# Weaving the weight tiles of three stages column by column, so that weight loads read with a step

## The chip, the cores and the metric

The kernel runs on one core of a Trainium2 chip. The metric is the time of one execution in microseconds of device time, the median of three runs. One profiled execution of the same kernel gives the trace that the views below are taken from.

Engines are named as in the profile: PE is TensorE with its matmuls, PEld is TensorE's weight loads (they overlap the matmuls), DVE is VectorE, ACT is ScalarE, POOL is GpSimd, SP is the sync engine, which issues the weight transfers.

## The reference

Two residual layers over 256 tokens of width 2048, in float32. The first has a mixer of Fourier and gated linear attention, the second a mixer of dilated attention. Each ends with a gated feed-forward part of inner width 5632, and these feed-forward parts are where the change lies:

```python
D_MODEL, SEQ, DEPTH, D_FF = 2048, 256, 2, 5632

def conv_ffn(xn, w_gate, w_up, conv_w, conv_b, w_down):
    g = xn @ w_gate
    g = lax.conv_general_dilated(g, conv_w[:, None, :], window_strides=(1,),
                                 padding=[(1, 1)], dimension_numbers=('NWC', 'WIO', 'NWC'),
                                 feature_group_count=D_FF) + conv_b
    h = jax.nn.gelu(g) * (xn @ w_up)
    return h @ w_down

def reference(x, ...):
    h = x
    for layer in range(DEPTH):
        xn = rms_norm(h, mix_norm_g[layer])
        h = h + (fourier_gla_mixer if layer % 2 == 0 else dilated_mixer)(xn, ...)
        h = h + conv_ffn(rms_norm(h, ffn_norm_g[layer]), ...)
    return h
```

## The kernel before

All weights come as one stream of tiles of 128x128 values, here called slots, in the order in which the program uses them. In device memory 16 slots lie side by side as a unit of 128 partitions x 2048 values; one transfer of 1 MB on SP's queue brings a unit into a `raw` tile. A unit is then split in two halves of eight slots each: ACT rounds a half to the short float32 format of TensorE (`hi`, line 119) and DVE takes the remainder (`lo`, line 120). So a half of eight slots is a pair of tiles `hi` and `lo` of 128 x 1024 values, and a slot is 128 neighbouring columns of each. `Stream.take` hands out a slot (or four at once) and runs the transfers and the splits ahead of use.

The stages in the order of the stream, with their slots: q0 64, z0 4, k0 64, a0 and v0 128 each, g0 128, o0 256, u0 1408 (gate and up projection of the first layer), d0 704 (down projection of the first layer), then the four blocks of q1, k1 and v1 with 768 together, o1 256, u1 1408 and d1 704 (the second layer's feed-forward part). That makes 6020 slots.

There are two kinds of matmul loop. In `mov` (stages a0, v0, q1, k1, v1) four slots of weights are the moving operand. In `stat` (all the others but z0) one slot is the stationary operand: it is loaded into the array, and the activations move. An activation operand of 128 x 512 values holds the rounded values of 256 tokens and their remainders; `pairs` reads it as columns c and c+256 in turn, that is, successive values lie 256 values (1 KB) apart. For every slot `stat` makes a matmul of `hi` with all 512 columns (line 337) and one of `lo` with the 256 columns of the rounded values (line 323). The second ones are held back in a list and sent off when the stream is at a multiple of 16 slots:

```python
                        if self.st.at % 16 == 0:
                            flush()
                        hi, lo = self.st.take(mat, k, j)
                        x = operand(k)
                        nc.tensor.matmul(ps[j], hi, self.pairs(x), start=k == k0, stop=False)
                        late.append(lower(ps[j], lo, x, k == k1))
```

So TensorE does 16 matmuls of 512 columns in a row, and then 16 of 256 columns, each with a weight load of 128 columns of its own. Stage z0 is a loop of its own (lines 462 and 463) with weight loads of 32 columns, and the attention of the second layer has matmuls whose moving operand is 256 neighbouring values (lines 895 and 936). `spread` (line 306) has a stationary operand that is one column repeated 128 times.

The order of the work is set by the order of the program and by the pools (three `raw` tiles, three `hi`, four `lo`, five accumulators). `pack` builds the stream's array ahead of the launch, outside of the time that is measured.

Of the kernel before, what the change touches and what calls it, by code (L numbers as in the profile page):

```python
# [14 lines left out]
P = 128  # L15
# [8 lines left out]
SLOT = 128  # L24
# [36 lines left out]
def slots_of(groups):  # L61
    return [(m, k, j) for m, js, ch in groups for c in ch for j in js for k in c]


def slots_of_block(mat, b):
    return [(mat, k, 4 * b + j) for k in range(KT) for j in range(4)]


def stream_slots():
    s = slots_of(Q0)  # L70
    s += [("z0", k, 0) for k in range(4)]
    s += slots_of(K0)
    for m in ("a0", "v0"):
        for b in range(2):
            s += slots_of_block(m, b)
    s += slots_of(G0) + slots_of(O0) + slots_of(U[0]) + slots_of(DN[0])
    for b in range(4):
        for m in ("q1", "k1", "v1"):
            s += slots_of_block(m, b)
    s += slots_of(O1) + slots_of(U[1]) + slots_of(DN[1])  # L80
    return s


class Stream:


# [3 lines left out]
    def __init__(self, k, src):  # L90
        self.k, self.src = k, src
        self.slots = stream_slots()
        self.at = 0
        self.halves = -(-len(self.slots) // 16) * 2
        self.raws = []
        self.ready = []
# [26 lines left out]
    def take(self, mat, kk, j, n=1):  # L123
        assert self.slots[self.at] == (mat, kk, j), (self.slots[self.at], mat, kk, j)
        half, off = divmod(self.at, 8)
        assert off + n <= 8
        if off == 0 and half > 0:
            self.k.side_step()
        while len(self.ready) < min(half + 1 + self.AHEAD, self.halves):
            self.split_next()  # L130
        hi, lo = self.ready[half]
        self.at += n
        s = slice(off * SLOT, (off + n) * SLOT)
        return hi[:, s], lo[:, s]


# [856 lines left out]
def shape_constants():  # L993
    i = np.arange(P)
    tri = np.stack([i[:, None] <= i[None], i[:, None] >= i[None], i[:, None] == i[None]], 1)
    lev = np.stack(
        [
            (i[:, None] // (2 * w) == i[None] // (2 * w)) & (i[:, None] // w != i[None] // w)
            for w in LEVELS
        ],  # L1000
        1,
    )
    n = np.arange(T)
    ang = 2 * np.pi * ((n[:, None] * n[None]) % T) / T
    cs = np.concatenate([np.cos(ang)[:, 0:129], np.sin(ang)[:, 1:128]], 1)
    dft = [m.reshape(2, P, -1) for m in (cs, np.cos(ang)[:, 0:P] / T, np.sin(ang)[:, 0:P] / T)]
    dft = np.concatenate([m.transpose(1, 0, 2).reshape(P, -1) for m in dft], 1)
    d = np.arange(512) - (T - 1)
    hot = np.arange(32)[:, None] == t5_bucket(d)[None]
    count = (np.abs(d) <= 64).astype(int) + (d % 4 == 0) + (d % 16 == 0)  # L1010
    cnt = np.where(count > 0, np.log(np.maximum(count, 1)), -1e30)
    return {
        "tri": tri.astype(np.float32),
        "lev": lev.astype(np.float32),
        "dft": dft.astype(np.float32),
        "hot": hot.astype(np.float32),
        "cnt": np.ascontiguousarray(np.broadcast_to(cnt, (16, 512))).astype(np.float32),
    }


def cols(v):

    return np.asarray(v).reshape(-1, P).T


def pack(inp):
    inp = {k: np.asarray(v) for k, v in inp.items()}
    w_in = inp["w_in_even"][0]
    w_qkv = inp["w_qkv_odd"][0]
    mirror = np.concatenate([np.arange(P), [P], np.arange(T - 1, P, -1)])  # L1030
    order = np.concatenate([g * T + mirror for g in range(4)] + [np.arange(1024, D)])
    mats = {
        "a0": w_in[:, 0:1024], "q0": w_in[:, 1024:1536], "k0": w_in[:, 1536:2048],
        "v0": w_in[:, 2048:3072], "g0": w_in[:, 3072:4096], "o0": inp["w_out_even"][0][order],
        "q1": w_qkv[:, 0:2048], "k1": w_qkv[:, 2048:4096], "v1": w_qkv[:, 4096:6144],
        "o1": inp["w_out_odd"][0], "d0": inp["w_down"][0], "d1": inp["w_down"][1],
    }
    for i in range(2):
        mats[f"u{i}"] = np.stack(
            [inp["w_gate"][i].reshape(D, FT, P), inp["w_up"][i].reshape(D, FT, P)], 2  # L1040
        ).reshape(D, 2 * FF)
    z = w_in[:, 4096:4128].reshape(4, 4, P, 32).transpose(0, 2, 1, 3).reshape(4 * P, P)
    mats["z0"] = z
    slots = stream_slots()
    w = np.zeros((-(-len(slots) // 16) * 16, P, SLOT), np.float32)
    tiles = {m: a.reshape(-1, P, a.shape[1] // P, P) for m, a in mats.items()}
    for s, (m, k, j) in enumerate(slots):
        w[s] = tiles[m][k, :, j]
    w = np.ascontiguousarray(w.reshape(-1, 16, P, SLOT).transpose(0, 2, 1, 3)).reshape(-1, P, UNIT)
    gates = np.zeros((33, 1024), np.float32)  # L1050
    gates[0:16, 0:512] = inp["gate_up_fwd"][0]
    gates[16:32, 512:1024] = inp["gate_up_bwd"][0]
    gates[32, 0:512] = inp["gate_bias_fwd"][0]
    gates[32, 512:1024] = inp["gate_bias_bwd"][0]
    par = np.concatenate(
        [
            cols(inp["mix_norm_g"]), cols(inp["ffn_norm_g"]), cols(inp["gla_norm_g"]),
            cols(inp["q_norm_g"]), cols(inp["k_norm_g"]),
        ],
        1,  # L1060
    )
    conv = np.concatenate([inp["conv_w"], inp["conv_b"][:, None]], 1)
    conv = conv.reshape(2, 4, FT, P).transpose(3, 0, 2, 1)
    x = inp["x"][0].T.reshape(KT, P, T).transpose(1, 0, 2)
    arrays = {"w": w, "gates": gates, "par": par, "conv": conv, "x": x, "rel": inp["rel_bias"]}
    arrays.update(shape_constants())
    return {k: np.ascontiguousarray(v) for k, v in arrays.items()}
# [29 lines left out]
```

## Time and profile before

| what | value |
|---|---|
| median of 3 runs | 2077.5 us (2077.2 to 2077.78) |
| the profiled execution, its own time | 2077.91 us |
| span of its trace | 2075.5 us |
| PE, PEld, DVE, ACT busy | 100%, 90%, 71%, 54% of the span |
| granted TensorE clock | 1.0 |
| weight transfers, share of 16 DMA engines | 53.9% |

The trace gives each instruction a start and an end. The ends of matmuls are modelled and overlap the next matmul, so what a matmul costs in a row of equal ones is read from one start to the next, not from its duration. Weight loads run beside the matmuls in the same way.

### The profile page before, as it was taken

How to read it: one execution, taken by the hardware profiler on the slowest of the kernel's cores; microseconds unless marked ns; L12 is line 12 of the kernel's file. 1: busy time of each engine (PE TensorE's matmuls, PEld its weight loads, DVE VectorE, ACT ScalarE, POOL GpSimd, SP SyncE). 2: the span in 40 equal slices, each digit the busy share in tenths (PEclk: the TensorE clock that was granted, in tenths of full speed). 3: DMA queues.
4: the chain of work that ended last, by engine and by line, in shares of the span. 5: the costliest groups of instructions: out<-in, count | busy, mean ns of one | idle time of the engine just before them, and what ended most of it. 6: DMA issues, size and time to landing. Idle time of an engine off the chain costs nothing.

```text
span 2075.5 us, 30467 instructions
## 1 busy us (share of the span) xinstructions
PE 2065.7 (100%) x12226; PEld 1876.8 (90%) x12226; DVE 1474.0 (71%) x2268; ACT 1125.8 (54%) x1623; POOL 22.1 (1%) x28
## 2 busy tenths in 40 slices
PE   8999999999999999999999999999999999999999
PEld 7898999999999999999888888999999999999998
DVE  7696777777777775655676777778777777765554
ACT  6765555555555554444455555556555555554443
POOL 3000000000000000000000000000000000000000
PEclk9999999999999999999999999999999999999999
DMA  7433555555555555555655455555555555555564
GB/s 273 162 142 127 198 203 188 202 202 203 203 203 203 198 200 198 200 200 202 232 184 197 178 178 188 180 192 200 201 202 203 203 203 201 199 200 211 206 212 151
DMA packets 60409, 406.28 MB, mean 196 GB/s; under 512 B 6875, under 2 KB 9435, under 8 KB 12524
## 3 DMA queue, kind: packets, MB, share of 16 engines
q1 hardware_dynamic: 56924, 398.93, 53.9%
q0 software_dynamic: 896, 3.28, 0.5%
q8 instruction: 95, 1.56, 0.3%
q10 hardware_dynamic: 2448, 2.13, 0.3%
q14 instruction: 46, 0.38, 0.0%
HBM read 402.19 MB, written 2.13 MB: 195 GB/s over the span
## 4 chain that ended last, share of the span: by engine, by line
PE 97%; ACT 1%; issue 0%; DVE 0%; DMA 0%; SPq 0%; DVEq 0%; ACTq 0%
PE acc L337 51%; PE acc L323 26%; PE acc L354 5%; PE acc L355 5%; PE acc L353 5%; PE ax L553 1%; PE ax L895 1%; PE ax L936 1%; PE ax L921 0%; PE ax L871 0%; ACT hi L119 0%; PE ax L688 0%; PE ax L621 0%; DMA raw<-in_w 0%; DVE page L254 0%
## 5 line engine op out<-in xcount | busy, mean ns | idle before, releaser
L120 DVE TENSOR_TENSOR lo<-raw,hi 128x1024 fp32r<-128x1024 f32 (+1 forms) x755 | 925.5, 1226 | 431.2 <-ACT hi L119 427.3
L337 PE MATMUL acc<-page,hi 128*128 128x512 f32 x4992 | 1136.4, 380 | 4.2 <-ACT hi L119 2.6
L119 ACT CAST hi<-raw 128x1024 fp32r<-128x1024 f32 (+1 forms) x755 | 791.9, 1050 | 510.3 <-PE acc L337 366.9
L337 PEld LDWEIGHTS acc<-page,hi 128*128 128x128 f32 x4992 | 918.6, 189 | 126.6 <-ACT hi L119 5.4
L323 PEld LDWEIGHTS acc<-page,lo 128*128 128x128 f32 x4992 | 607.2, 192 | 17.2
L323 PE MATMUL acc<-page,lo 128*128 128x256 f32 x4992 | 609.1, 275 | 0.0
L353 PE MATMUL acc<-hi,page 128*128 128x512 f32 x512 | 197.1, 385 | 0.0
L354 PE MATMUL acc<-lo,page 128*128 128x512 f32 x512 | 194.1, 379 | 0.3 <-DVE lo L120 0.3
L355 PE MATMUL acc<-hi,page 128*128 128x512 f32 x512 | 194.0, 379 | 0.0
L750 ACT ACTIVATE c<-t,conv 128x256 f32<-128x256 f32 x88 | 52.8, 600 | 155.4 <-DVE t L748 155.4
L220 ACT CAST page<-t 128x256 fp32r<-128x256 f32 x96 | 38.8, 405 | 152.3 <-DVE t L765 151.6
L355 PEld LDWEIGHTS acc<-hi,page 128*128 128x128 f32 x512 | 96.8, 189 | 13.7
L354 PEld LDWEIGHTS acc<-lo,page 128*128 128x128 f32 x512 | 96.8, 189 | 13.1 <-DVE lo L120 0.6
L353 PEld LDWEIGHTS acc<-hi,page 128*128 128x128 f32 x512 | 96.8, 189 | 12.5
L751 DVE SCALAR_TENSOR_TENSOR c<-t,conv,c 128x255 f32<-128x255 f32 x88 | 42.6, 484 | 56.3 <-ACT c L750 56.3
L362 DVE TENSOR_TENSOR t<-acc,t 128x256 f32<-128x256 f32 (+1 forms) x193 | 80.3, 417 | 0.0
L361 ACT COPY t<-acc 128x256 f32<-128x256 f32 (+1 forms) x193 | 71.0, 369 | 3.5 <-PE acc L323 2.7
L221 DVE TENSOR_TENSOR page<-t,page 128x256 fp32r<-128x256 f32 x96 | 40.6, 424 | 38.6 <-ACT page L220 38.6
L253 ACT ACTIVATE page<-hT,par 128x256 fp32r<-128x256 f32 x64 | 31.8, 506 | 38.8 <-DVE hT L729 38.2
L760 ACT ACTIVATE gr<-c 128x256 f32<-128x256 f32 x88 | 36.7, 417 | 15.7 <-DVE c L755 15.6
L755 DVE SCALAR_TENSOR_TENSOR c<-t,conv,c 128x255 f32<-128x255 f32 x88 | 42.6, 484 | 3.1
L254 DVE SCALAR_TENSOR_TENSOR page<-hT,par,page 128x256 fp32r<-128x256 f32 x64 | 34.4, 547 | 7.3 <-ACT page L253 7.3
(160 smaller groups left out, 803.0 us busy)
## 6 DMA issues: line engine op xcount, KB each, us to landing
raw<-in_w SPq DMA_DIRECT2D x373, 1024.0 KB, 4.8
raw<-in_w SPq DMA_DIRECT2D x7, 512.0 KB, 7.3
page<-brow POOLq DMA_DIRECT2D x4, 768.0 KB, 5.7
out<-hT ACTq DMA_DIRECT2D x16, 128.0 KB, 2.9
hT<-in_x SPq DMA_DIRECT2D x7, 256.0 KB, 7.4
raw<-in_w SPq DMA_DIRECT2D x2, 256.0 KB, 3.4
page<-in_dft SPq DMA_DIRECT2D x1, 512.0 KB, 6.3
page<-in_lev SPq DMA_DIRECT2D x1, 448.0 KB, 5.4
```

Of the source, the lines that this page charges most:

```text
L119: k.nc.scalar.copy(hi[:, c], part[:, c])
L120: k.nc.vector.tensor_sub(lo[:, c], part[:, c], hi[:, c])
L323: return lambda: nc.tensor.matmul(ps[:, 0:T], lo, self.pairs(x)[:, 0:P], start=False, stop=last)
L337: nc.tensor.matmul(ps[j], hi, self.pairs(x), start=k == k0, stop=False)
L353: nc.tensor.matmul(ps[t], xh, hi, start=k == 0, stop=False)
L354: nc.tensor.matmul(ps[t], xh, lo, start=False, stop=False)
L355: nc.tensor.matmul(ps[t], xl, hi, start=False, stop=k == KT - 1)
L361: self.nc.scalar.copy(v, self.unpaired(ps[0:rows, T:512]))
L362: self.nc.vector.tensor_add(v, self.unpaired(ps[0:rows, 0:T]), v)
L750: nc.scalar.activation(c, t, AF.Identity, scale=w(1), bias=w(3))
L751: nc.vector.scalar_tensor_tensor(out=c[:, 1:T], in0=t[:, 0 : T - 1], scalar=w(0), in1=c[:, 1:T], op0=ALU.mult, op1=ALU.add,)
L755: nc.vector.scalar_tensor_tensor(out=c[:, 0 : T - 1], in0=t[:, 1:T], scalar=w(2), in1=c[:, 0 : T - 1], op0=ALU.mult, op1=ALU.add,)
```

## The change

For three stages the slots that lie side by side in a half are woven in groups of g: two in u0, four in d0, eight in u1. A group of g slots takes the same g x 128 columns as before, but column c of slot i now lies at place c x g + i in the group. `places` gives for each slot the first slot of its group, the group's size and the slot's place in it. Where a stage starts or ends within a half (u1 does so with four slots at either end) the group is smaller. `take` returns for a single slot a view with a step of g values, `pack` writes the array in this order. All the other stages have groups of one, with a step of one as before. The bytes moved, the splits by ACT and DVE, which work on whole halves, and the instructions of all engines with their order are the same as before; what differs is the step with which the weight loads of lines 337 and 323 (354 and 340 in the changed file) read in u0, d0 and u1.

```diff
+WOVEN = {"u0": 2, "d0": 4, "u1": 8}
+
+def places(slots):
+    out = []
+    for s, (m, _, _) in enumerate(slots):
+        n = WOVEN.get(m, 1)
+        group = [i for i in range(s // n * n, s // n * n + n) if slots[i][0] == m]
+        out.append((group[0], len(group), s - group[0]))
+    return out
...
         self.slots = stream_slots()
+        self.places = places(self.slots)
...
         hi, lo = self.ready[half]
+        first, g, i = self.places[self.at]
         self.at += n
-        s = slice(off * SLOT, (off + n) * SLOT)
+        first = first % 8 * SLOT
+        s = slice(first + i, first + g * SLOT, g) if n == 1 else slice(first, first + n * SLOT)
         return hi[:, s], lo[:, s]
...
         w[s] = tiles[m][k, :, j]
+    for first, g, i in places(slots):
+        if g > 1 and i == 0:
+            part = w[first : first + g].transpose(1, 2, 0).reshape(P, g, SLOT)
+            w[first : first + g] = part.transpose(1, 0, 2)
```

## The prediction

> **What bounds the kernel now.** I read the totals first, then the slices, the costliest groups, the timeline of TensorE, and a table by stage.
>
> ```profile
> PE 2065.7 (100%) x12226; PEld 1876.8 (90%) x12226; DVE 1474.0 (71%) x2268; ACT 1125.8 (54%) x1623; POOL 22.1 (1%) x28
> ...
> PEclk9999999999999999999999999999999999999999
> ...
> PE 97%; ACT 1%; issue 0%; DVE 0%; DMA 0%; SPq 0%; DVEq 0%; ACTq 0%
> ...
> L120 DVE TENSOR_TENSOR lo<-raw,hi 128x1024 fp32r<-128x1024 f32 (+1 forms) x755 | 925.5, 1226 | 431.2 <-ACT hi L119 427.3
> L337 PE MATMUL acc<-page,hi 128*128 128x512 f32 x4992 | 1136.4, 380 | 4.2 <-ACT hi L119 2.6
> ...
> L337 PEld LDWEIGHTS acc<-page,hi 128*128 128x128 f32 x4992 | 918.6, 189 | 126.6 <-ACT hi L119 5.4
> L323 PEld LDWEIGHTS acc<-page,lo 128*128 128x128 f32 x4992 | 607.2, 192 | 17.2
> L323 PE MATMUL acc<-page,lo 128*128 128x256 f32 x4992 | 609.1, 275 | 0.0
> ```
>
> TensorE carries 97% of the chain at full clock. It waits 4.2 us in all ahead of 4992 hi matmuls and never ahead of the lo ones. Transfers and splits are in time, so only what TensorE does per slot counts. That is read from starts, here in u0 (start, duration, count of a merged run):
>
> ```profile
> 601.52 1.95 PE L323 MATMUL acc<-page,lo 128*128 128x256 f32 x16
> 603.31 3.62 PE L337 MATMUL acc<-page,hi 128*128 128x512 f32 x16
> 606.76 1.95 PE L323 MATMUL acc<-page,lo 128*128 128x256 f32 x16
> 608.55 3.62 PE L337 MATMUL acc<-page,hi 128*128 128x512 f32 x16
> ```
>
> Sixteen slots take 606.76 - 601.52 = 5.24 us, 327.5 ns a slot. What share a hi matmul has is seen best where matmuls of 512 columns stand alone, in the second mixer; the same rows give the price of a moving operand of neighbours:
>
> ```profile
> 1081.51 0.38 PE L353 MATMUL acc<-hi,page 128*128 128x512 f32 x1
> ...
> 1084.10 0.88 PE L936 MATMUL ax<-page,page 128*128 128x256 f32 x6
> 1084.81 0.60 PE L921 MATMUL ax<-tri,t 128*128 128x128 f32 x4
> ```
>
> From 1081.51 to 1084.10 there are twelve matmuls of 512 columns: 215.8 ns each. So a lo matmul in u0 takes 327.5 - 215.8 = 111.7 ns. The stage z0 has the same two matmuls per step, moved the same way, but loads 32 columns of weights instead of 128:
>
> ```profile
> 32.02 0.38 PE L462 MATMUL acc<-page,hi 128*32 128x512 f32 x1
> ...
> 36.57 0.38 PE L462 MATMUL acc<-page,hi 128*32 128x512 f32 x1
> ```
> ```profile
> L462 PEld LDWEIGHTS acc<-page,hi 128*32 128x32 f32 x16 | 1.8, 109 | 1.5
> L306 PEld LDWEIGHTS ax<-tri,rs_y 128*128 128x128 f32 x16 | 2.2, 190 | 0.4 <-ACT hi L119 0.4
> ```
>
> Fourteen steps take 4.55 us, 325.0 ns each, so 109.2 ns for the 256 columns when the load is short. The loads of 32 and 128 columns differ by 189 - 109 = 80 ns, 0.83 ns a column, 106.7 ns for 128. So two things are true of a lo run: the matmuls need 109.2 ns, the loads behind them need 111.7 (106.7 and 5 of their own), and the load sets the pace by 2.5 ns. In a hi run the load of 111.7 ns lies under 215.8 ns of matmul, with 104 ns to spare.
>
> **The change part by part.** The same instructions stand in the same order on every engine; the bytes, the transfers and the whole-half splits of lines 119 and 120 are as before. These cost nothing because nothing in them changes; no cover is needed. The weaving itself is done ahead of the launch. One term is left: the time of a weight load that reads with a step of 2, 4 or 8 values. How often it counts, by stage (u0, d0, u1, and d1, which stays as it is):
>
> ```profile
> core 0: us, PE busy (x) PEld busy (x) DVE busy (x) ACT busy (x) POOL busy (x), PEclk, DMA share, GB/s
> 314.40:777.40 463.00, 463.00 (x2827) 424.30 (x2826) 356.64 (x542) 261.71 (x396) 0.86 (x2) 1.00 0.57 201
> 777.50:1008.00 230.50, 230.50 (x1410) 211.62 (x1410) 132.16 (x154) 105.24 (x122) 1.56 (x2) 1.00 0.57 205
> 1379.10:1841.00 461.90, 461.90 (x2826) 424.17 (x2825) 356.02 (x541) 261.55 (x396) 0.00 (x0) 1.00 0.57 201
> 1841.10:2075.00 233.90, 230.69 (x1410) 211.63 (x1408) 120.53 (x126) 93.32 (x91) 0.00 (x0) 1.00 0.56 197
> ```
>
> The three stages hold 1408 + 704 + 1408 = 3520 slots (1408 x 327.5 ns = 461.1 us, near the 463.0 and 461.9 of the table). Half of their 7040 loads, the hi ones, can grow by 104 ns unseen. The other half has no cover at all: each ns more costs 3520 x 1 ns = 3.5 us, each ns less gains as much, but only down to the 109.2 ns of the matmul.
>
> The trace of before has no weight load with a step above one, so the price has to be bounded.
> - From below: the matmul's floor. At most 2.5 ns x 3520 = 8.8 us are gained: 2068.7 us.
> - At zero: two rows speak for it. The load in line 306 reads one and the same column 128 times (a step of zero) and takes 190 ns like the loads of neighbours with 189 and 192, so the load's time is not that of fetching neighbours. And the moving operand of z0 and u0 is read in turns from places 1 KB apart, 256 values in 109.2 ns, 0.43 ns a value: a step from value to value that is faster than the 0.83 ns that the load needs.
> - From above: line 936 moves 256 neighbours and takes 0.71 us / 6 = 118.3 ns, 9.1 ns more than the same count read in turns from two places. That looks like fetches of several neighbours at the limit of what a read can get, with the reading in turns as a way around it. If a fetch holds four values, one takes 118.3 / 64 = 1.85 ns. Then a load with a step of 4 or 8 needs 128 fetches, 236.6 + 5 = 241.6 ns, and one with a step of 2 needs 64, 123.3 ns. Lo runs: 2112 x (241.6 - 111.7) = 274.3 us in d0 and u1, 1408 x 11.6 = 16.3 in u0; hi runs: 2112 x (241.6 - 215.8) = 54.5. Sum 345 us: 2422 us.
>
> I take zero: reading in turns is the nearest row that has a step and the only one that runs faster than a load has to, and the row with step zero is the nearest that is a load. The sum is 0 on the profiled execution's 2077.91 us (span 2075.5 and 2.4 around it). That execution stands 0.4 us above the median of the runs, so I forecast the median, 2077.5 us.
>
> [...]
>
> **The rivals.**
> 1. The step makes loads shorter, as reading in turns made moving shorter (118.3 to 109.2). Then lo runs go at the matmul's 109.2 ns, 3520 x 2.5 = 8.8 us less: 2069 us. For it: the load sets the pace of lo runs. Against: the load with a step of zero is no shorter, and 0.83 ns a column is slower than any read shown here, so the load's pace seems to be that of filling the array.
> 2. A fetch holds two neighbours and is at its limit at 118.3 / 128 = 0.92 ns, or the two readers of TensorE get in each other's way a little. Then each woven load reads 128 fetches: 123.3 ns, 11.6 more. 3520 x 11.6 = 40.8 us: 2118 us, with 2085 to 2160 for smaller or larger losses of that kind.
> 3. Slower by far, the case on the other side: where a load uses one value of each fetch (d0 and u1), a value takes two column steps instead of one, so 106.7 ns more a load. Lo runs: 2112 x 106.7 = 225.3 us. Hi runs: a load of 218.4 passes the 215.8 of the matmul, 2112 x 2.6 = 5.5 us. Sum 230.8: 2308 us. It decides from 1.2 ns more per lo load on (4.2 us over 3520 loads). For it: line 936, which is slow with neighbours at 2.3 times the load's rate. Against: the reading in turns. Its worst form is the 2422 us above; if only a step of 8 suffers, 1408 x (106.7 + 2.6) = 154 us gives 2231.
>
> That nothing would happen because the step isn't there can be left out: the view that `take` returns is the operand itself.
>
> **How the numbers follow.** The step is free: 0.44, with 2073 to 2082 as its own range (a change of some 4 us, 0.2%, is about what can be told from none here). Rival 1: 0.12. Rival 2: 0.14. Rival 3 at 2231 to 2308: 0.24, and its worst form 0.06. So faster has 0.12, same 0.44, slower 0.14 + 0.24 + 0.06 = 0.44. The predicted time is that of the free step, 2077.5 us, the likeliest single case. As slower cases together weigh as much, the range goes from rival 1's 2069 to rival 3's 2308 with a little above, 2310; the worst form stays out.
>
> **What would show each step right or wrong.** If the step is free, the runs of 16 lo matmuls stay at 1.79 us and those of 16 hi at 3.45 in all three stages, weight loads at 189 to 192 ns, and the stages at 463.0, 230.5 and 461.9 us. In rival 1 the lo runs go to 1.75 us, and u0 and u1 lose 3.5 us each. In rival 2 they go to 1.97 us. In rival 3 u0 keeps its 463 us, the loads of d0 and u1 last near 296 ns, their lo runs take 3.49 us, d0 grows to about 307 us and u1 to about 616. In each case d1 and all stages outside of the three must take what they took; if d1 moves too, it isn't the step. The forecast is wrong if the reads of a load, unlike those of the moving operand, can't take successive values from different places at one per 0.83 ns.

## The result, and the profile after

The changed kernel takes 2407.0 us (median of 4 runs, 2406.1 to 2407.5) against 2077.4 us before (the three runs of above and a fourth): a ratio of 1.158, interval 1.157 to 1.160, 329.6 us more. The profiled execution has 2406.59 us, 328.7 more than the one of before. The forecast of 2077.5 us was wrong, and the time lies outside of its range too.

The totals and the costliest groups of the changed kernel, in the order of the page (lines 354 and 340 were 337 and 323):

```profile
PE 2394.8 (100%) x12226; PEld 2272.3 (94%) x12226; DVE 1478.2 (61%) x2268; ACT 1137.9 (47%) x1623; POOL 22.0 (1%) x28
...
PEclk9999999999999999999999999999999999999999
...
PE acc L354 47%; PE acc L340 34%; PE acc L371 5%; PE acc L372 5%; PE acc L370 5%; PE ax L570 1%; PE ax L912 1%; PE ax L953 0%; PE ax L888 0%; PE ax L938 0%; ACT hi L134 0%; PE ax L705 0%; PE ax L638 0%; DMA raw<-in_w 0%; DVE page L271 0%
...
L354 PEld LDWEIGHTS acc<-page,hi 128*128 128x128 f32 x4992 | 1058.5, 254 | 68.9 <-ACT hi L134 5.6
L340 PEld LDWEIGHTS acc<-page,lo 128*128 128x128 f32 x4992 | 878.1, 254 | 8.6
```

TensorE still carries 98% of the chain, at full clock. The mean weight load went from 189 and 192 ns to 254, and the lo matmuls from 26% of the chain to 34%. The table by stage (u0, d0, u1, and the untouched d1) says where:

```profile
314.50:789.70 475.20, 475.20 (x2829) 446.44 (x2828) 358.03 (x542) 268.24 (x396) 0.99 (x3) 1.00 0.55 196
789.80:1120.60 330.80, 330.80 (x1410) 330.80 (x1408) 132.61 (x154) 105.67 (x122) 1.56 (x2) 1.00 0.41 147
1491.80:2170.10 678.30, 678.30 (x2826) 678.27 (x2824) 359.68 (x542) 267.71 (x397) 0.00 (x0) 1.00 0.39 138
2170.30:2404.00 233.70, 230.75 (x1409) 211.68 (x1408) 119.78 (x124) 92.29 (x90) 0.00 (x0) 1.00 0.55 194
```

u0 grew from 463.0 to 475.2 us, d0 from 230.5 to 330.8, u1 from 461.9 to 678.3: 12.2 + 100.3 + 216.4 = 328.9 us, which is all of the 328.7 between the two profiled executions. d1 has 233.7 against 233.9. In d0 and u1 the weight loads are busy for the whole stage: they, and no longer the matmuls, are the bound of the hi runs as well. In the timeline (u0, then d0, then u1):

```profile
600.27 3.62 PE L354 MATMUL acc<-page,hi 128*128 128x512 f32 x16
603.73 2.08 PE L340 MATMUL acc<-page,lo 128*128 128x256 f32 x16
605.65 3.63 PE L354 MATMUL acc<-page,hi 128*128 128x512 f32 x16
```
```profile
900.75 4.05 PE L354 MATMUL acc<-page,hi 128*128 128x512 f32 x16
904.64 3.80 PE L340 MATMUL acc<-page,lo 128*128 128x256 f32 x16
908.28 4.05 PE L354 MATMUL acc<-page,hi 128*128 128x512 f32 x16
```
```profile
1802.80 3.90 PE L340 MATMUL acc<-page,lo 128*128 128x256 f32 x16
1806.54 4.13 PE L354 MATMUL acc<-page,hi 128*128 128x512 f32 x16
1810.51 3.90 PE L340 MATMUL acc<-page,lo 128*128 128x256 f32 x16
```

With a step of two, lo runs take 1.92 us, 120 ns a load, and hi runs stay at 3.46. With a step of four, 32 loads take 7.53 us, 235 ns each, with hi and lo runs nearly alike; with a step of eight 7.71 us, 241 ns each. In these two stages a matmul of 256 or of 512 columns now costs nearly the same, since both wait for a load that is longer than either (109 and 216 ns before).

### The profile page after: what moved, and what is told of

It is laid out like the page before. It is cut to its first block, busy times and chain, and to the rows that moved or that the text cites. A ratio compares the mean times of both kernels' runs of the same rounds, so it can differ in the third digit from the quotient of the medians.

```text
span 2404.8 us, 30467 instructions
## 1 busy us (share of the span) xinstructions
PE 2394.8 (100%) x12226; PEld 2272.3 (94%) x12226; DVE 1478.2 (61%) x2268; ACT 1137.9 (47%) x1623; POOL 22.0 (1%) x28
## 4 chain that ended last, share of the span: by engine, by line
PE 98%; ACT 1%; issue 0%; DVE 0%; DMA 0%; SPq 0%; DVEq 0%; ACTq 0%
PE acc L354 47%; PE acc L340 34%; PE acc L371 5%; PE acc L372 5%; PE acc L370 5%; PE ax L570 1%; PE ax L912 1%; PE ax L953 0%; PE ax L888 0%; PE ax L938 0%; ACT hi L134 0%; PE ax L705 0%; PE ax L638 0%; DMA raw<-in_w 0%; DVE page L271 0%
## 5 line engine op out<-in xcount | busy, mean ns | idle before, releaser
L354 PE MATMUL acc<-page,hi 128*128 128x512 f32 x4992 | 1201.4, 393 | 4.4 <-ACT hi L134 2.8
L354 PEld LDWEIGHTS acc<-page,hi 128*128 128x128 f32 x4992 | 1058.5, 254 | 68.9 <-ACT hi L134 5.6
L340 PEld LDWEIGHTS acc<-page,lo 128*128 128x128 f32 x4992 | 878.1, 254 | 8.6
L340 PE MATMUL acc<-page,lo 128*128 128x256 f32 x4992 | 873.3, 328 | 0.0
L782 DVE TENSOR_TENSOR t<-t,gr 128x256 f32<-128x256 f32 x88 | 37.4, 425 | 2.9
```

The costliest lines, as they stand in the source:

```text
L340: return lambda: nc.tensor.matmul(ps[:, 0:T], lo, self.pairs(x)[:, 0:P], start=False, stop=last)
```

## The experiments

The loads of a step of two and four differ by 115 ns. If a load fetches pieces of four neighbouring values (16 bytes), 128 values with a step of two lie in 64 pieces and with a step of four in 128. They then differ by 64 fetches, 1.8 ns each. That was theory A. The rivals were a threshold (a step of 16 bytes or more is slow, a smaller one is not; theory B) and a memory bank that steps which are powers of two hit over and over (theory C).

The edits below are shortened; a line in words stands for the code that does it. The kernel with only u0 woven was run four times, each of the others once; the kernel before, run along with them, took 2078.1, 2077.9 and 2077.1 us.

**All steps, stages exchanged.**

```diff
-WOVEN = {"u0": 2, "d0": 4, "u1": 8}
+sizes of the groups in a half of eight slots:
+    u0: 8    d0: 2,2,2,2    u1: 5,3    d1: 4,4    o0: 3,3,2    o1: 7,1    g0: 6,2
```

> All steps from 1 to 8 in one kernel, and the stages exchanged: u0 step 8, d0 step 2, d1 step 4, u1 halves of five slots with step 5 and three with step 3, o0 groups of 3, 3, 2, o1 of 7 and 1, g0 of 6 and 2. Theory A (a weight load fetches pieces of four neighbouring values, 1.8 ns each, and takes 5 ns + 1.8 ns x fetches where that is above 111.5): lo pace by step 119.6 ns (2, 64 fetches), about 178 (3, 96 fetches), 227 to 240 for every step from 4 on (128 fetches), whatever the stage; d0 about 236 us, u0 about 678, d1 about 331; whole kernel about 2624 us. Theory B (a step of 16 bytes or more doubles the time of a column, below that little): step 3 near 120 like step 2, whole kernel about 2582 us. Theory C (steps that are powers of two fall on one bank): steps 3, 5 and 7 near 112 to 125, only 2, 4, 8 (and in part 6) slow, about 2430 us.

It took 2600.8 us. The mean of the lo loads by stage, in the order g0, o0, u0, d0, o1, u1, d1:

```profile
L351 PEld LDWEIGHTS acc<-page,lo 128*128 128x128 f32 x128 | 26.1, 286 | 0.2
...
L351 PEld LDWEIGHTS acc<-page,lo 128*128 128x128 f32 x256 | 43.4, 246 | 0.3
...
L351 PEld LDWEIGHTS acc<-page,lo 128*128 128x128 f32 x1408 | 346.4, 337 | 0.0
...
L351 PEld LDWEIGHTS acc<-page,lo 128*128 128x128 f32 x704 | 91.6, 199 | 1.7
...
L351 PEld LDWEIGHTS acc<-page,lo 128*128 128x128 f32 x256 | 57.0, 310 | 0.4
...
L351 PEld LDWEIGHTS acc<-page,lo 128*128 128x128 f32 x1408 | 298.5, 297 | 0.0
...
L351 PEld LDWEIGHTS acc<-page,lo 128*128 128x128 f32 x704 | 168.9, 330 | 0.0
```

Steps 2, 4 and 8 give 199, 330 and 337 ns, here in d0, d1 and u0 as in u0, d0 and u1 of the changed kernel: the step decides, not the stage. (These are durations, which overlap; the pace of the loads is shorter.) From o0's mix, (6 x 262 + 2 x 199) / 8 = 246, step 3 has 262 ns. From u1's mix, (5 x 318 + 3 x 262) / 8 = 297, step 5 has 318. From g0's, (6 x 315 + 2 x 199) / 8 = 286, step 6 has 315. From o1's, (7 x 327 + 192) / 8 = 310, step 7 has 327. So step 3 lies halfway between 2 and 4, as its 96 fetches lie between 64 and 128; theory B's threshold would have left it near 199. Steps 5 and 7 (318 and 327 ns) are nearly as slow as 4 and 8, so theory C falls. The stages u0, d0 and d1 took 679.4, 236.4 and 330.8 us, where theory A had said 678, 236 and 331. Its sum for the whole kernel was 23 us too high; steps 5 and 6 turned out a little quicker than 4 and 8, which theory A doesn't explain.

**Short lo matmuls.**

```diff
-                ps[:, 0:T], lo, self.pairs(x)[:, 0:P], start=False, stop=last
+                ps[:, 0 : 2 * n], lo, self.pairs(x)[:, 0:n], start=False, stop=last
+    with n = P if last else 16
```

> The weave of the changed kernel, but every lo matmul except the last of an accumulation moves 32 columns instead of 256; most of the lo product is left out. The lo pace is then the weight load alone. If the load sets the pace, as read from the trace before, the lo runs of unwoven stages stay at 111.5 ns. Theory A with a load that is limited by its own fetches: 119.6 (u0), 227 (d0) and 233 (u1) stay. If instead the load and the moving operand take each other's fetches: below that, at most 111.5 in u0 and about 218 (two column steps of 0.83 ns a value, and 5) or less in d0 and u1.

It took 2636.3 us. A row each of lo runs and the run behind it, in the unwoven o0, then u0 and u1:

```profile
282.73 1.85 PE L352 MATMUL acc<-page,lo 128*128 128x32 f32 x16
284.43 3.70 PE L366 MATMUL acc<-page,hi 128*128 128x512 f32 x16
...
604.37 1.95 PE L352 MATMUL acc<-page,lo 128*128 128x32 f32 x16
606.16 2.20 PE L366 MATMUL acc<-page,hi 128*128 128x512 f32 x9
```
```profile
1801.18 3.78 PE L352 MATMUL acc<-page,lo 128*128 128x32 f32 x16
1804.80 5.27 PE L366 MATMUL acc<-page,hi 128*128 128x512 f32 x16
1809.91 3.77 PE L352 MATMUL acc<-page,lo 128*128 128x32 f32 x16
```

Of the sixteen intervals of a run, the first is short, since the run's first matmul starts late, behind the last hi matmul: by the trace's starts 0.03 us in o0 and u0, 0.05 in u1. (In the kernel before, a run of four matmuls of one column starts at 190.44, its second at 190.47, and the run behind it at 190.80: 0.03 us, then 110 ns a load.) The other fifteen are loads: (1.70 - 0.03) / 15 = 111 ns in o0, 117 in u0, and (3.62 - 0.05) / 15 = 238 in u1. An eighth of the moving columns changes nothing in o0: the load does set the pace of lo runs, as the prediction read it. And a stepped load is slow by itself; it isn't waiting for fetches of the moving operand. That this kernel is slower than the changed one has another cause, told at the end.

**Only u0 woven.**

```diff
-WOVEN = {"u0": 2, "d0": 4, "u1": 8}
+WOVEN = {"u0": 2}
```

> Only u0 woven (two together); d0 and u1 as before. If the costs of the stages add up: u0 475 us, d0 230.5, u1 461.9, and the time 2077.4 + 12.0 = 2089.4 us. If u0's loss came from the slow stages behind it: 2077.

It took 2090.5 us against 2078.1 for the kernel before, a ratio of 1.0064 (interval 1.0048 to 1.0081). The row of u0:

```profile
314.50:789.50 475.00, 475.00 (x2826) 446.62 (x2826) 357.97 (x542) 268.09 (x396) 0.83 (x2) 1.00 0.54 196
```

u0 takes 475.0 us, d0 230.4 and u1 461.9: the costs of the stages add up, and a step of two alone loses 12 us.

**The moving operand as neighbours.** Why did the moving operand not show this price? Its reading in turns had been my nearest row. In this kernel the activations lie as 256 rounded values and then 256 remainders, and are read in that order.

```diff
-        v = x.rearrange("p (a z c) -> p z a c", a=2, z=2)
+        v = x.rearrange("p (z a c) -> p z a c", a=2, z=2)
...
-  hi matmul: self.pairs(x)    lo matmul: self.pairs(x)[:, 0:P]
+  hi matmul: x                lo matmul: x[:, 0:T]
```

> No weave; instead the moving operand of all stat stages is read as neighbours, no longer in turns from two places 1 KB apart. If the 118.3 ns of line 936 is the price of 256 neighbours for any moving operand (64 fetches at about 1.8 ns): lo pace 118, hi pace about 234, 4992 x 25 = 124 us more, about 2201 us. If line 936's price comes from its own place (accumulations of three, attention around it): 111.5 and 216 as before, 2077 us.

It took 2180.3 us.

```profile
602.82 2.08 PE L331 MATMUL acc<-page,lo 128*128 128x256 f32 x16
604.74 3.82 PE L345 MATMUL acc<-page,hi 128*128 128x512 f32 x16
608.39 2.08 PE L331 MATMUL acc<-page,lo 128*128 128x256 f32 x16
```

256 neighbours take 1.92 / 16 = 120 ns, 512 take 228. The 118.3 ns of line 936 was a price of reading neighbours, not of that line's place in the kernel. The hi runs lose less than the 234 ns expected.

**The moving operand with a step of two, and of four.**

```diff
-        v = x.rearrange("p (a z c) -> p z a c", a=2, z=2)
+  two:  v = x.rearrange("p (a c z) -> p z a c", a=2, z=2)    read: "p (c z) -> p z c", z=2
+  four: v = x.rearrange("p (c z a) -> p z a c", a=2, z=2)    read: "p (c w) -> p w c", w=4
```

> No weave of the weights; the activations are laid out with rounded value and remainder side by side, so that the moving operand of all stat stages reads with a step of two (8 bytes). Theory A for the moving operand too (one fetch of four neighbours per 1.8 ns, as the runs with loads and with neighbours showed, and 2.5 ns a matmul): 256 columns are 128 fetches, 233 ns; 512 columns are 256, 463 ns. A slot 696 ns instead of 327.5: 4992 x 368 = 1840 us more, about 3920 us. Theory D (what costs is a port that only loads have; the moving operand takes successive values from any place, as the reading in turns from places 1 KB apart does without loss): 111.5 and 216, 2077 us. The mov stages load with a step of two here: 120 ns, hidden under 216.

> As the kernel with a moving step of two, with a step of four (16 bytes): every value is in a piece of its own, and the piece has been left four times when its last value is read. Theory A: 256 fetches for 256 columns, 463 ns, and 512 for 512, 924 ns; a slot 1387 ns, 4992 x 1060 = 5290 us more; the loads of the mov stages with a step of four add 1536 x 19 = 29 us; about 7400 us. A price that only halves the rate from a step of 16 bytes on: 216 and 430 ns, 4992 x 318, about 3670 us. Theory D: 2077 us and 29 for the loads of mov.

They took 3839.7 and 3949.0 us. The timeline of the first, then of the second:

```profile
800.57 7.40 PE L345 MATMUL acc<-page,hi 128*128 128x512 f32 x16
807.78 3.81 PE L331 MATMUL acc<-page,lo 128*128 128x256 f32 x16
811.41 3.79 PE L345 MATMUL acc<-page,hi 128*128 128x512 f32 x8
```
```profile
800.70 7.57 PE L345 MATMUL acc<-page,hi 128*128 128x512 f32 x16
808.08 3.92 PE L331 MATMUL acc<-page,lo 128*128 128x256 f32 x16
811.82 3.42 PE L345 MATMUL acc<-page,hi 128*128 128x512 f32 x7
```

A step of two costs 227 ns for 256 columns, 451 for 512; a step of four 234 and 461. So theory D falls: a stepped moving operand pays as well, and takes more than double the time. But theory A in its simple form falls for it too: from step two to four the fetches double and the time grows by 2 to 3%. The loads of the mov stages, whose stationary operand is now the activations, read with the same steps and take 196 and 331 to 334 ns, close to the woven weights of u0 and d0: the price of a stepped load isn't tied to the weight tiles. For the moving operand the times suggested two readers that take successive values by turns (theory E): each would see one value per piece at either step, 128 fetches each, and in the order of before four neighbours per piece.

**Two near places, four places.** The activations lie as in the kernel with neighbours, and are read in blocks:

```diff
+  two near:    x.rearrange("p (b s q) -> p b q s", s=2, q=4)     0, 4, 1, 5, 2, 6, 3, 7
+  four places: x.rearrange("p (b s q) -> p b q s", s=4, q=4)     0, 4, 8, 12, 1, 5, 9, 13, ...
```

> No weave; the moving operand of all stat stages is read in turns from two places only 16 bytes apart: in blocks of eight values the order 0, 4, 1, 5, 2, 6, 3, 7. Theory E (the moving operand is read by two readers that take successive values by turns; each fetches a piece of four neighbours in about 1.8 ns and holds one piece): each reader sees four neighbours in a row, 32 fetches for 256 columns, so the matmul's own pace: 111.5 and 216 ns, about 2077 us. Rival F (reading in turns is fast because the two places are far apart): the near places lose as neighbours do or more, 119.5 and 228 (2180 us) up to 230 and 455 (3840 us).

> As the kernel with two near places, with four places by turns: in blocks of 16 the order 0, 4, 8, 12, 1, 5, 9, 13 and so on. No piece of four neighbours is used less than whole. Theory E: each reader sees two pieces by turns (0, 8, 1, 9), so every value is a fetch of its own, 128 for 256 columns: 230 to 233 ns, and 455 to 461 for 512, as with the moving steps of two and four; about 3840 to 3950 us. Rival G (what counts is how many values of each fetched piece are used in the end, since a few pieces are held): 111.5 and 216, about 2077 us.

They took 2076.95 and 2454.9 us. Two near places, then four:

```profile
601.13 1.95 PE L343 MATMUL acc<-page,lo 128*128 128x256 f32 x16
602.91 3.62 PE L357 MATMUL acc<-page,hi 128*128 128x512 f32 x16
606.37 1.84 PE L343 MATMUL acc<-page,lo 128*128 128x256 f32 x15
```
```profile
600.69 2.33 PE L343 MATMUL acc<-page,lo 128*128 128x256 f32 x16
602.85 4.46 PE L357 MATMUL acc<-page,hi 128*128 128x512 f32 x16
607.15 2.33 PE L343 MATMUL acc<-page,lo 128*128 128x256 f32 x16
```

Two places 16 bytes apart are as good as two 1 KB apart, 111 and 216 ns; between these two the distance makes no difference, and rival F falls. Four places cost 135 and 269 ns. That is neither E's 230 nor G's 111.5. Theory E's readers, which hold a single piece each, are refuted by it. What stands is that 256 values take 109 to 120 ns where four neighbours are used within eight reads, 135 where they are used within sixteen, and 227 to 234 where the reads go on after one or two of them. Whether the moving operand is fetched in pieces of four at all, how many would be held, and what the four places lose, stays open.

## Why the prediction was wrong

**What bounds the kernel** was right: a stage's time is TensorE's, lo runs go at the pace of their loads (111 ns with short matmuls too), and hi runs have room for a longer load. u0 shows the latter: loads of 120 ns cost it nothing in hi runs, which stay at 3.46 us.

**That nothing but the step counts** was right: d1 kept its time, and the growth of the three stages, 328.9 us, leaves nothing of the 328.7 us between the profiled executions for any other.

**The step that failed is "I take zero".** It was chosen because reading in turns from places 1 KB apart was "the nearest row that has a step". It is not a row with a step in the sense that matters. How far successive values lie apart doesn't set the price: in the kernel with two near places the distance is 16 bytes instead of 1 KB, and a lo matmul takes 111 ns as before. For the loads the price went with how many of four neighbours are used: all four at a step of one (111.5 ns), two at a step of two (120), one at a step of four or eight (235 and 241). Reading in turns uses all four. Instead of 0 the term of the stepped loads was 12.2 us in u0, 100.3 in d0 and 216.4 in u1. The row with a step of zero was no witness either: a load that fetches few pieces may be hidden behind the filling of the array, which the prediction put at 0.83 ns a column, as one of neighbours is. No run separates the two there.

**The upper bound was the price.** It was worked out from line 936: 1.85 ns a fetch of four neighbours, loads of 123.3 and 241.6 ns, 345 us in all. Measured: 1.8 ns (115 ns over 64 fetches), 120 ns in u0, 235 in d0, 241 in u1, and 329 us. By term: u0 16.3 expected by it, 12.2 measured; d0 and u1 together 274.3 + 54.5 = 328.8 expected, 316.7 measured. I gave that form 0.06, and left it outside of the range. That its size came so near is in part luck. It takes a piece's price from a moving operand, and for those the runs don't show one price a piece: four places touch the same 64 pieces as neighbours do and take 135 ns instead of 120. Rival 3's larger sum, two column steps a value (218.4 ns, 2308 us), was too low: that a value takes two steps was my estimate, which no run shows; the loads took 235 and 241 ns, 1.8 ns a fetch and not 1.67, and u0, which it put at nothing, lost 12.2 us. Rival 2's 123.3 ns is near the size for u0 alone, and its fetches of two neighbours don't fit d0. Its other cause, two readers in each other's way, is not what the short lo matmuls show: with an eighth of the moving columns the loads of u0 and u1 still take 117 and 238 ns. One figure in rival 3 is wrong, and nothing hangs on it: line 936 takes its 256 values in 118.3 ns, 0.46 ns a value, which is 1.8 times the load's rate and not 2.3.

**Four values a fetch** was a supposition, which no row of before shows. The loads of the runs fit it: with steps of 2, 3 and 4 they last 199, 262 and 330 ns, and with 8 no more than 337. Two values a piece are not quite enough for the pace of a step of one: u0's loads take 120 ns instead of 111.5. I took zero for the moving operand's sake. But the runs show that operand to pay a price too: at a step of two, 256 values take 227 ns instead of 109.

## What to carry to other kernels

Count, for a float32 weight load like those here, the pieces of four neighbouring values that it touches, not the distance from one value to the next: with 32, 64 and 128 pieces (steps of one, two and four) the loads took 111.5, 120 and 235 ns, and with a step of eight, 128 pieces again, 241. From 64 pieces on, each more costs about 1.8 ns (115 ns over 64). By that, the 32 pieces of 128 columns in a row need some 58 ns (an estimate, 32 x 1.8), which doesn't show beside the 111 ns that such a load takes; a step of two costs 8 ns, and a step of four or eight doubles the load. For a moving operand such a count is not shown: 64 pieces took 109 ns from two places by turns, 120 as neighbours and 135 from four places. When a bound from a row and a chosen value lie 345 us apart, look for an argument that tells the rows apart before giving one of them 0.06; here line 936 and the reading in turns already contradicted any account in which distance alone decides.

## What the runs showed of the hardware beyond that

Reading the moving operand with a step of two costs nearly as much as with a step of four (451 against 461 ns for 512 columns). Steps of five and six are a little cheaper for loads than steps of four and eight (durations of 318 and 315 against 330 and 337 ns); why stays open.

The kernel with short lo matmuls lost part of its clock. The clock in 40 slices, and its u0, d0 and u1:

```profile
PEclk9999999999998777779999996777777777778999
...
317.60:789.20 471.60, 471.60 (x2827) 443.63 (x2825) 348.62 (x542) 263.34 (x398) 0.49 (x1) 1.00 0.55 197
789.40:1196.60 407.20, 407.20 (x1408) 371.20 (x1408) 132.43 (x153) 105.12 (x122) 1.56 (x2) 0.74 0.33 119
1569.40:2398.00 828.60, 828.60 (x2824) 759.21 (x2824) 352.23 (x541) 259.63 (x398) 0.00 (x0) 0.75 0.32 113
```

Where matmuls of 32 columns stand between loads with a step of four or eight (238 ns each in u1), the mean granted clock is 0.74 and 0.75, though TensorE counts as busy throughout. The hi run shown above takes 1809.91 - 1804.80 = 5.11 us there instead of 3.97. In u0, with loads of 117 ns, the same short matmuls keep the clock at 1.0. d0 and u1 take 407.2 - 330.8 = 76.4 and 828.6 - 678.3 = 150.3 us longer than in the changed kernel, 226.7 of the 229.3 us that this kernel is slower. It is one run, and by which rule the clock falls stays open.
